# Two accumulations of the index queries use another PSUM bank

## The chip, the cores and the metric

The kernel runs on one core of a Trainium2 chip. The metric is the device time of one execution in microseconds (us), as the median of several runs. TensorE (PE below) does the matmuls, VectorE is DVE, ScalarE is ACT, GpSimd is POOL and SyncE is SP, from whose queue the transfers (DMAs) are issued. PSUM, where matmuls accumulate, has eight banks of 128 x 512 float32.

## The reference

One layer of a mixer on a sequence of 1024 rows of width 1024. After a layer norm `h`, one projection feeds four groups, A (spatial gating), B (band attention), C (sparse attention) and M (attention into 256 memory rows); each is multiplied by its SiLU gate, and an output projection and a last layer norm follow. What the change touches is the indexer of group C:

```
proj = x @ w_in + b_in          # ... iq: 8 heads of 64 columns, ik: 64 columns, iw: 8
logits = jnp.einsum('bqhd,bsd->bqhs', iqb, ikf) * (IDX_DIM ** -0.5)
score = jnp.einsum('bqhs,bqh->bqs', jax.nn.relu(logits), iwb * (IDX_HEADS ** -0.5))
_, idx = lax.top_k(score, k_sel)      # 256 keys for each query
```

The eight index heads are handled as four pairs, since two heads of 64 columns fill the 128 partitions. Below, "pair 1" to "pair 4" are the values 0 to 3 of `j` in the code.

## The kernel before, in words

Every projection is made by `project` (line 212): the weights `t` and the transposed input are each kept as a high and a low part, and for each of eight slices of the inner dimension there are three matmuls, high by high, high by low and low by high. So one piece of output columns is 24 matmuls of 512 (or 256) columns, accumulated in one PSUM bank, a tile `acc`. `wblock` (line 194) loads a block of weights; ACT makes the high part and POOL subtracts it for the low part (line 208).

The eight PSUM banks are divided by `BANKS` (line 68): two for `pp` (projections), two for `qk` and three for `pt` (scores and transposes), and one for `pv`, the value products of the attention. In the early stage there are no value products, and `pv` also serves a few other things: the SiLU projections of group A's gates (line 491), the transposed index weights (`iwt`, line 504) and the transposed spatial weights (`wst`, line 785), which ACT then copies into the tile `atab`.

The index queries: `iq_tile` (line 457) loads the weights of a pair and calls `parts_half` (line 343) for the columns 256 to 512 (the shorter piece) and then 512 to 1024 (the longer piece). `parts_half` projects, and then copies the sum out of PSUM: ACT writes the high part `iqh`, DVE the low part `iql`. Both are tiles of the tag `s4`, of which there are eight buffers (line 65), shared with `ikh`, `ikl`, `v3m`, `km`, `atab` and others; a tile gets a buffer when an earlier one has had its last reader. `index_heads` (line 464) makes the scores of a pair, row block by row block (2 and 3 together, then 4, 5, 6 and 7): 64-row matmuls `qk` of the two heads at once, ACT's relu into one of four `S` buffers, and DVE's weighted sum into `score`. `INDEX_ORDER` (line 56) is "h0 q2 h1 q3 h2 h3": the scores of pair 1, the queries of pair 3, the scores of pair 2, the queries of pair 4, then the scores of pairs 3 and 4. The queries of pairs 1 and 2 come before that. After the index part the program has `wst`, the definitions of the attention, and the gates of A (`gate_of_a`, line 487: GELU in `pp`, SiLU in `pv`, twice for each of two blocks) with the first steps of the search for the 256 largest scores.

That is the program's order. The order in which each engine takes its instructions is laid out when the kernel is built: instructions are taken by priority (the place in the program, or raised as by `BOOST_Q` for the copies of the index queries) as they become ready in a modelled time, so that later work fills the holes of earlier work. On the chip each engine then keeps to that order and waits on semaphores.

Of the kernel before, what the change touches and what calls it, by code (L numbers as in the profile page):

```python
# [24 lines left out]
P = 128  # L25
# [16 lines left out]
BOOST_Q = 2000  # L42
# [22 lines left out]
S4, EV, WB, SB, BOOST = 8, 4, 5, 4, 400  # L65
# [5 lines left out]
C_Q, C_K, C_V, C_G, I_Q, I_K, I_W, M_Q, M_G = 1792, 2048, 2304, 2560, 2816, 3328, 3392, 3400, 3656  # L71


def f32(ap):
    return ap.bitcast(F32)
# [3 lines left out]
def tile_trunk(ctx, tc, x, mem, ln_in_g, ln_in_b, w_in, b_in, a_ln_g, a_ln_b, a_ws, a_bs,  # L79
# [25 lines left out]
    def run(steps):  # L105

        while True:
            try:
                next(steps)
            except StopIteration as e:  # L110
                return e.value
# [58 lines left out]
    def s4(name, dt=F32R, shape=(P, SEQ)):  # L170
        return gp.tile(list(shape), dt, tag="s4", bufs=S4, name=name)
# [16 lines left out]
    def bank(tag, name=None):  # L188
        return ps.tile([P, 512], F32, tag=tag, bufs=BANKS[tag], name=name or tag)
# [4 lines left out]
    def wblock(w, c0, m=P):  # L194

        raw = E.tile([P, KT, P], F32, tag="raw", bufs=2, name="raw")
        loads.append(SP.dma_start(out=raw[:, :, :m], in_=w[:, c0:c0 + m].rearrange("(k p) c -> p k c", p=P)).ins)
        ts = []
        if m < P:
            narrow = [gp.tile([P, 2, KT // 2, m], F32R, tag=tag, bufs=1, name="wnar") for tag in ("planes", "score6")]  # L200
        for q in range(2):
            t = E.tile([P, 2, 4, P], F32R, tag="w", bufs=WB, name="wblk") if m == P else narrow[q]
            r = raw[:, 4 * q:4 * q + 4, :m]
            if WH[0] <= len(loads) < WH[1]:
                G.tensor_scalar(t[:, 0], r, 1.0, 0.0, ALU.mult, ALU.add)
            else:
                S.activation(t[:, 0], r, AF.Copy)
            G.tensor_sub(t[:, 1], r, f32(t[:, 0]))  # L208
            ts.append(t)
        return ts  # L210

    def project(t, a, b, m=P, hi=hh, lo=hl, tag="pp"):

        acc = bank(tag, "acc")
        for k in range(KT):
            wh, wl = t[k // 4][:, 0, k % 4, :m], t[k // 4][:, 1, k % 4, :m]
            PE.matmul(acc[:m, :b - a], wh, hi(k, a, b), start=(k == 0), stop=False)
            PE.matmul(acc[:m, :b - a], wh, lo(k, a, b), start=False, stop=False)
            PE.matmul(acc[:m, :b - a], wl, hi(k, a, b), start=False, stop=(k == KT - 1))
            yield  # L220
        return acc
# [118 lines left out]
            g = silu_of(acc, col[c0])  # L340
        SP.dma_start(out=gate_dram[kt][i], in_=g)

    def parts_half(t, c0, parts, a, b, boost=BOOST):

        hi, lo = parts
        acc = yield from project(t, a, b)
        n, bc = b - a, bias[:, col[c0]:col[c0] + 1]
        with tc.high_priority(offset=boost):
            S.activation(hi[:, a:b], acc[:, :n], AF.Identity, bias=bc)
            V.scalar_tensor_tensor(lo[:, a:b], acc[:, :n], bc, f32(hi[:, a:b]), ALU.add, ALU.subtract)  # L350
# [106 lines left out]
    def iq_tile(j):  # L457
        t = wblock(w_in, I_Q + j * P)
        q = [s4("iqh"), s4("iql")]
        for a, b in ((256, 512), (512, 1024)):  # L460
            run(parts_half(t, I_Q + j * P, q, a, b, BOOST_Q))
        return q

    def index_heads(j, q):
# [31 lines left out]

    table_parts = table_loads()
    iqs = [iq_tile(0)]
    with tc.issue_after(loads[-1]):
        for rb in range(NB):  # L500
            SP.dma_start(out=h_dram[rb], in_=xts[rb])
    tables(*table_parts)
    iqs.append(iq_tile(1))
    ptw = bank("pv", "iwt")
    for rb in range(NB):
# [12 lines left out]
    for what, j in INDEX_ORDER.split():  # L518
        j = int(j)
        if what == "q":  # L520
            iqs.append(iq_tile(j))
        if what == "h":
            index_heads(j, iqs[j])
        run(gates_of(f"{what}{j}"))
        if what == "h" and j == 3:
            for rb in RBS:
                V.memset(score[rb][0:64, (rb + 1) * P - 64:(rb + 1) * P], LOW)
# [65 lines left out]
    def parts_of(items):  # L593

        n = len(items)
        parts = []
        for t in range(n + 3):
            now, prev, prev2, prev3 = [items[t - d] if 0 <= t - d < n else None for d in range(4)]
            if now:
                parts.append(now.scores)  # L600
            if prev2:
                parts.append(prev2.values[-1])
            if prev:
                parts.append(prev.turn[0])
            if prev3 and prev3.close:
                parts.append(prev3.close)
            if prev:
                for turn, values in zip(prev.turn[1:], prev.values):
                    parts += [turn, values]
        return parts  # L610
# [156 lines left out]
    def queries_of_m(pair, q):  # L767
        wmq = wblock(w_in, M_Q + pair * P)
        q += [s4("mqh"), s4("mql")]
        for a, b in HALVES:  # L770
            yield from parts_half(wmq, M_Q + pair * P, q, a, b)
# [85 lines left out]
    class Pair:  # L857
# [13 lines left out]
        def piece(self, what, half):  # L871
            w, c = self.weight(what), self.c["qkvg".index(what)]
            if what == "q":
                if not hasattr(self, "q"):
                    self.q = [s4("qh"), s4("ql")]
                yield from parts_half(w, c, self.q, *HALVES[half])
            if what == "k":
                if not hasattr(self, "k"):
                    self.k = [s4("kh"), s4("kl")]
                yield from parts_half(w, c, self.k, *HALVES[half])  # L880
            if what == "g":
                yield from gate_half(w, c, self.kt, half)
            self.turn()
            if what == "v":
                if not hasattr(self, "v3"):
                    self.v3 = gp.tile([P, NB, 2, 3, 64], BF16, tag="v3", bufs=2, name="v3")
                acc = yield from project(w, *HALVES[half])
                with tc.high_priority(offset=BOOST):
                    vT = ev("vT")
                    S.activation(vT, acc, AF.Identity, bias=bias[:, col[c]:col[c] + 1])  # L890
                self.turned.append((vT, half))
# [410 lines left out]
    parts = parts_of(items)  # L1302
# [80 lines left out]
```

## Time and profile before

| | us |
|---|---|
| median of 3 runs | 677.58 |
| lowest, highest | 675.11, 680.07 |
| the profiled execution | 678.19 |
| its span, from the first to the last instruction | 676.4 |

| engine | busy us | share of the span | instructions |
|---|---|---|---|
| PE | 638.7 | 94% | 3698 |
| DVE | 480.1 | 71% | 1165 |
| ACT | 426.4 | 63% | 947 |
| POOL | 354.4 | 52% | 354 |

Shares are averages over stages with different limits. Matmuls follow each other in a pipeline, so that durations of single ones overlap; the spacing of their starts is what counts. A number in brackets behind an instruction in a timeline is the time for which its engine was idle before it, with what ended the idle time. The granted clock (PEclk) is 1.00 at 2.4 GHz and 0.50 at 1.2 GHz.

### The profile page before, as it was taken

To read this page: it belongs to the slowest core of one execution; us is meant where nothing else is said; L and a number is where in the kernel's file an instruction comes from. 1 tells how busy PE (TensorE), PEld (TensorE's weight loads), DVE (VectorE), ACT (ScalarE), POOL (GpSimd) and SP (SyncE) were. 2 spreads that over 40 slices of the span, in tenths; PEclk is the share of its full clock that TensorE was granted. 3 is DMA by queue.
4 is the path that set the end of the run, shared out by engine and by line. 5 is a ranking of instruction groups with operands and counts; after the bars stand their busy time and mean duration, and the time that the engine had idled before them with its cause. 6 is when DMAs were issued, how large, how long until landed. Compare 5 with 4: busy or idle time off the path is not lost.

```text
span 676.4 us, 11066 instructions
## 1 busy us (share of the span) xinstructions
PE 638.7 (94%) x3698; PEld 484.5 (72%) x3698; DVE 480.1 (71%) x1165; ACT 426.4 (63%) x947; POOL 354.4 (52%) x354
## 2 busy tenths in 40 slices
PE   4889999899999999989998999999999999999995
PEld 3867776677787677767665776667677777778785
DVE  6584256567867789899889778995567559787535
ACT  4665255547599998776879986466456575356210
POOL 3682321104535886484448535994214776557851
PEclk9999999899999999999999999999999999999999
DMA  9783521012234543554347625645101574225111
GB/s 280 236 296 112 163 57 32 0 48 63 78 110 94 110 117 97 115 123 135 71 101 139 148 74 110 120 82 150 31 16 44 180 230 145 72 88 193 66 62 63
DMA packets 121669, 75.30 MB, mean 111 GB/s; under 512 B 58976, under 2 KB 111500, under 8 KB 121612
## 3 DMA queue, kind: packets, MB, share of 16 engines
q1 hardware_dynamic: 121612, 74.59, 40.5%
q8 instruction: 29, 0.48, 0.3%
q14 instruction: 28, 0.23, 0.1%
HBM read 46.44 MB, written 17.64 MB: 95 GB/s over the span
## 4 chain that ended last, share of the span: by engine, by line
PE 50%; DVE 13%; POOL 11%; ACT 11%; issue 8%; DMA 6%; SPq 0%; POOLq 0%; DVEq 0%; ACTq 0%
PE acc L94 36%; PE qk L94 6%; ACT jka L94 4%; PE pv L94 4%; POOL wblk L208 3%; DMA pT<-sc 3%; PE pt L94 2%; DVE jk L94 2%; POOL sc L545 2%; ACT sc L94 1%; DMA raw<-in_w_in 1%; POOL sc L546 1%; DVE sc L94 1%; DMA xt<-in_x 1%; DMA hr<-h_dram 1%
## 5 line engine op out<-in xcount | busy, mean ns | idle before, releaser
L94 PE MATMUL acc<-hTh,wblk 128*128 128x512 f32 (+1 forms) x960 | 317.4, 400 | 6.4 <-DVE iql L94 2.6
L94 PEld LDWEIGHTS acc<-hTh,wblk 128*128 128x128 f32 x960 | 177.2, 189 | 52.5 <-issue 6.1
L94 PE MATMUL acc<-hTl,wblk 128*128 128x512 f32 (+1 forms) x480 | 190.4, 397 | 0.0
L208 POOL TENSOR_TENSOR wblk<-raw,wblk 128x512 fp32r<-128x512 f32 x72 | 99.7, 1388 | 123.2 <-ACT wblk L94 120.0
L94 ACT ACTIVATE jka<-score,cand 128x768 int8<-128x768 f32 (+2 forms) x93 | 96.5, 1038 | 16.2 <-DVE cand L94 15.4
L94 PEld LDWEIGHTS acc<-hTl,wblk 128*128 128x128 f32 x480 | 90.9, 189 | 20.6 <-issue 4.0
L94 PEld LDWEIGHTS <-pT 128*128 128x128 f16 x656 | 45.7, 98 | 31.7 <-issue 17.9
L94 DVE SCALAR_TENSOR_TENSOR score<-relu,iw,score 128x384 f32<-128x384 f32 (+5 forms) x42 | 43.7, 1058 | 23.9 <-ACT relu L94 22.1
L94 PE MATMUL pv<-v,pT 128*128 128x192 bf16 (+1 forms) x528 | 54.3, 234 | 4.8 <-DMA pT<-sc 4.0
L94 ACT ACTIVATE wblk<-raw 128x512 fp32r<-128x512 f32 x72 | 44.5, 627 | 22.6 <-PE acc L94 12.8
L546 POOL TENSOR_TENSOR sc<-sc 128x512 f16<-128x512 f32 (+4 forms) x48 | 56.0, 1172 | 2.3
L94 PE MATMUL acc<-woh,mh 128*128 128x512 f32 (+1 forms) x144 | 55.3, 384 | 0.0
L94 PE MATMUL acc<-wol,mh 128*128 128x512 f32 (+1 forms) x144 | 53.5, 372 | 0.0
L94 PE MATMUL acc<-woh,ml 128*128 128x512 f32 (+1 forms) x144 | 53.5, 373 | 0.0
L94 ACT ACTIVATE relu<-qk 128x384 f32<-128x384 f32 (+2 forms) x80 | 35.9, 530 | 24.1 <-PE qk L94 23.8
L545 POOL TENSOR_SCALAR sc<-sc 128x512 f16<-128x512 f32 (+4 forms) x48 | 33.4, 698 | 30.6 <-ACT sc L94 28.6
L94 ACT ACTIVATE sc<-sc,nb 128x640 f32<-128x640 f32 (+7 forms) x64 | 46.5, 729 | 1.2
L94 ACT ACTIVATE pT<-pt 128x512 f16<-128x512 f32 (+3 forms) x48 | 22.5, 485 | 31.0 <-PE pt L94 30.7
L94 ACT ACTIVATE o<-o,ri 128x64 f32<-128x64 f32 x96 | 28.1, 341 | 17.8 <-DVE o L94 17.6
L94 DVE TENSOR_SCALAR_CACHE_REDUCE jk<-planes,lo 128x384 bf16<-128x384 uint16 (+2 forms) x48 | 35.6, 742 | 1.1
L94 DVE TENSOR_SCALAR_CACHE_REDUCE jk<-planes,cand 128x384 bf16<-128x384 bf16 (+2 forms) x45 | 33.5, 744 | 1.1
L94 DVE TENSOR_REDUCE o<-pv 128x128 f32<-128x384 f32 x48 | 26.4, 549 | 9.7 <-PE pv L94 9.6
(204 smaller groups left out, 1238.4 us busy)
## 6 DMA issues: line engine op xcount, KB each, us to landing
raw<-in_w_in SPq DMA_DIRECT2D x32, 512.0 KB, 3.8
xt<-in_x SPq DMA_DIRECT2D x8, 512.0 KB, 4.7
h_dram<-xt SPq DMA_DIRECT2D x8, 512.0 KB, 5.6
gate<-t SPq DMA_DIRECT2D x16, 256.0 KB, 2.1
rawo<-in_w_out SPq DMA_DIRECT2D x8, 512.0 KB, 3.7
hr<-h_dram SPq DMA_DIRECT2D x8, 512.0 KB, 5.2
out<-hr SPq DMA_DIRECT2D x7, 512.0 KB, 2.6
gate<-gate SPq DMA_DIRECT2D x48, 64.0 KB, 2.1
```

What stands on the lines that cost most here:

```text
L94: ins = op(*a, **k)
L208: G.tensor_sub(t[:, 1], r, f32(t[:, 0]))
L545: G.tensor_scalar(high, sc[:, :n], 1.0, 0.0, ALU.mult, ALU.add)
L546: G.tensor_sub(rest, sc[:, :n], high)
```

## The change

The function `parts_half` gets an argument for the tag of the PSUM bank and hands it to `project`. `iq_tile` passes "pv" for the longer piece (`b > 512`) of the third and fourth pair (`j > 1`), and "pp", as before, for all others. Every other caller of `parts_half` keeps "pp".

```
-    def parts_half(t, c0, parts, a, b, boost=BOOST):
+    def parts_half(t, c0, parts, a, b, boost=BOOST, tag="pp"):
 
         hi, lo = parts
-        acc = yield from project(t, a, b)
+        acc = yield from project(t, a, b, tag=tag)
...
         for a, b in ((256, 512), (512, 1024)):
-            run(parts_half(t, I_Q + j * P, q, a, b, BOOST_Q))
+            run(parts_half(t, I_Q + j * P, q, a, b, BOOST_Q, "pv" if b > 512 and j > 1 else "pp"))
         return q
```

## Rows read from the trace of the kernel before

**Rows 1.** The page, parts 1 and 2: busy time, and busy tenths in 40 slices

```profile
PE 638.7 (94%) x3698; PEld 484.5 (72%) x3698; DVE 480.1 (71%) x1165; ACT 426.4 (63%) x947; POOL 354.4 (52%) x354
...
PE   4889999899999999989998999999999999999995
```

**Rows 2.** Waits of PE: who waited for whom, us in total, times, longest

```profile
PE pv L94 <- DMA pT<-sc: 5.4, 7, 1.4
PE acc L94 <- DVE iql L94: 2.6, 2, 2.1
```

**Rows 3.** Timeline of PE: start, us, instruction, count [idle before, releaser]

```profile
100.12 0.39 PE L94 MATMUL qk<-ikl,iqh 64*128 64x512 f32 x2
...
101.88 0.39 PE L94 MATMUL acc<-hTh,wblk 128*128 128x256 f32 x1 [0.58 <-DVE iql L94]
...
117.77 0.39 PE L94 MATMUL qk<-ikl,iqh 64*128 64x512 f32 x2
...
118.63 0.34 PE L94 MATMUL qk<-ikl,iqh 64*128 64x384 f32 x2
121.04 0.79 PE L94 MATMUL acc<-hTh,wblk 128*128 128x512 f32 x1 [2.07 <-DVE iql L94]
```

**Rows 4.** Windows: length, busy us (instructions) of each engine, PEclk, DMA

```profile
121.04:124.33 3.29, 3.29 (x8) 2.61 (x9) 3.29 (x4) 0.60 (x2) 0.00 (x0) 0.50 0.00 0
...
97.18:118.97 21.79, 21.14 (x140) 14.76 (x139) 13.04 (x15) 14.50 (x32) 3.85 (x3) 1.00 0.17 46
```

**Rows 5.** Windows by stage: PE, PEld, DVE, ACT, POOL, PEclk, DMA

```profile
130.00:146.00 16.00, 16.00 (x87) 11.62 (x87) 7.11 (x8) 8.21 (x18) 4.48 (x4) 1.00 0.13 34
183.00:250.00 67.00, 65.61 (x346) 51.05 (x346) 51.64 (x136) 63.45 (x144) 40.95 (x43) 1.00 0.46 113
250.00:400.00 150.00, 141.70 (x844) 104.83 (x843) 128.66 (x378) 124.09 (x288) 85.44 (x103) 1.00 0.49 112
400.00:640.00 240.00, 238.22 (x1428) 177.15 (x1427) 172.22 (x448) 135.50 (x323) 146.58 (x129) 1.00 0.38 108
```

**Rows 6.** Timeline of ACT: the copies of the queries of pairs 3 and 4

```profile
100.83 1.06 ACT L94 ACTIVATE iqh<-acc,bias 128x256 fp32r<-128x256 f32 x2
...
118.86 1.04 ACT L94 ACTIVATE iqh<-acc,bias 128x256 fp32r<-128x256 f32 x2
```

**Rows 7.** Timeline of DVE: the low parts of the same queries

```profile
101.34 1.33 DVE L94 SCALAR_TENSOR_TENSOR iql<-acc,bias,iqh 128x256 fp32r<-128x256 f32 x2
...
120.51 1.14 DVE L94 SCALAR_TENSOR_TENSOR iql<-acc,bias,iqh 128x256 fp32r<-128x256 f32 x2
```

**Rows 8.** Timeline of POOL: the last weights split before the gates of A

```profile
97.72 1.28 POOL L208 TENSOR_TENSOR wblk<-raw,wblk 128x512 fp32r<-128x512 f32 x1 [2.16 <-ACT wblk L94]
```

**Rows 9.** The chain that ended last, merged pieces: start, us, what, count

```profile
77.75 5.79 PE acc L94 x24
...
137.82 1.27 PE qk L94 x12
139.09 3.94 PE acc L94 x16
143.02 1.59 PE qk L94 x12
```

**Rows 10.** Timeline of PE: `wst`, and the first matmul of the first SiLU projection

```profile
96.76 0.49 PE L94 MATMUL wst<-ident,wsn 128*128 128x128 f32 x3
...
147.10 0.50 PE L94 MATMUL acc<-hTh,wblk 128*128 128x512 f32 x1
```

**Rows 11.** Timeline of ACT: the copy of `wst`

```profile
146.45 0.60 ACT L94 ACTIVATE atab<-wst 128x512 f32<-128x512 f32 x1 [0.43 <-PE qk L94]
```

**Rows 12.** Window of PE, matmuls that write `acc` alone

```profile
121.00:147.08 26.08, 19.63 (x72) 0.94 0.08 21
```

**Rows 13.** Timeline of DVE: pair 3's sums for row blocks 5 and 6

```profile
139.11 2.14 DVE L94 SCALAR_TENSOR_TENSOR score<-relu,iw,score 128x768 f32<-128x768 f32 x2 [2.12 <-ACT relu L94]
...
144.59 2.40 DVE L94 SCALAR_TENSOR_TENSOR score<-relu,iw,score 128x896 f32<-128x896 f32 x2 [3.33 <-ACT relu L94]
```

## The prediction

> **What bounds the kernel now.** I read the page's busy lines first, then the list of TensorE's waits, then the order of time around the index queries. The busy lines show TensorE (PE) at 638.7 us of a span of 676.4, and its row of slices at 8 or 9 tenths from the second slice on [rows 1]. So time comes back only where PE stands still or runs at its lower clock. The list of waits names a wait that belongs to the edited lines: PE, at an `acc` matmul, waits for the DVE instruction that writes `iql`, twice, 2.6 us in total, 2.1 the longest [rows 2].
>
> The PE timeline places the two: 0.58 us before the short piece of pair 4's queries at 101.88, and 2.07 us before the first GELU projection of the gates at 121.04 [rows 3]. Behind the second one the granted clock is 0.50 from 121.04 to 124.33 [rows 4]: 3.29 us at 1.2 GHz in place of 2.4, so half of it, 1.65 us, is lost. The place therefore costs 0.58 + 2.07 + 1.65 = 4.30 us. PE stands before it and after it without a hole: 16.00 of 16 us from 130 to 146, at 1.00 [rows 5].
>
> Why it waits: the two pieces of pair 3's queries fill both `pp` banks by about 97, but ACT copies them out (`iqh`, two at once) only at 100.83, and the pieces of pair 4 only at 118.86 [rows 6]. The copies go into tiles of the eight `s4` buffers. By the program's names eight are alive there (the two `ik` parts, `v3m`, `km`, the two parts of pairs 1 and 2), so pair 3's parts need the buffers of pair 1, which are read until that pair's last scores, and pair 4's those of pair 2. The times agree: by the order of the score groups pair 1's last ones start at 100.12 and pair 2's at 117.77 [rows 3]. DVE then frees the banks at 102.67 (101.34 + 1.33) and 121.65 (120.51 + 1.14), the ends of its two pairs of `iql` [rows 7]. So the banks are held by a buffer that is missing, and not by slow copies.
>
> **The change, part by part.** Matmuls, copies, tiles and DMAs are the same in number; no instruction is added, no queue (SP and POOL among them) gets another transfer or is passed by one. What moves is the bank of two 24-matmul accumulations, from `pp` to the one `pv` bank. After it the order of `pp` is pair 3 short (bank 0), pair 4 short (bank 1), first GELU (bank 0). Three consequences.
>
> *First wait.* Pair 4's short piece takes a bank that was emptied long before (pair 2's), and its weights and the next tile's are split by POOL by 99.0 (97.72 + 1.28) [rows 8]. It can run from 97 on, in the place where PE had nothing but scores and the transposes `wst`. The 0.58 goes. Its long piece must wait for `pv`, so until 102.67; ahead of that lie the last scores of pair 1, the short piece (half the columns of a long one, which takes 5.79 us for its 24 matmuls [rows 9], so 2.9) and pair 2's first scores: the scores now take from 97.18 to 101.30, where the hole begins (101.88 - 0.58) [rows 3], and 2.9 more end at 104.2. I cost that at nothing; without this cover at most 0.58 comes back.
>
> *Second wait.* The first GELU takes the bank of pair 3's short piece, free from about 102, and its weights are the tile split by 99.0 [rows 8]. It lasts 5.8 us as the long piece does and has only the copy-out of 102 ahead of it, in place of the one of 121. PE has work over the 2.07 us, and with the hole the spell of half clock should go as well. Together with the first: 4.30 back.
>
> *What is late next.* (a) `wst`, four transposes of the spatial weights in `pv`, began at 96.76 [rows 10]. It stands behind pair 4's long piece in the program, so it now runs after 121.65 and PE, which takes its order as written, can stand at it: from nothing to 121.65 - 118.97 = 2.68 us (118.63 + 0.34 being the end of the scores ahead of the hole [rows 3]). I take nothing, because the GELU's 5.8 us can lie ahead of it; the other end stays for a rival. What waits for `wst` is the copy into `atab`, and that runs at 146.45 in any case, since it needs an `s4` buffer of pair 3, free with that pair's last scores [rows 11]. (b) `pv` stays shut to the SiLU projection until then, so between 121 and 147 PE's filling is three GELU projections on `pp` and no more (72 `acc` matmuls, 3 x 24 [rows 12]); at 147.10, just behind the `atab` copy (146.45 + 0.60), the first SiLU begins [rows 10, 11]. The filling now starts earlier and ends earlier; if pair 3's scores don't move up by as much, PE runs dry ahead of them. Those scores are paced by DVE once the filling is gone: for row blocks 5 and 6 DVE takes 2.14 and 2.40 us [rows 13] where PE takes 1.27 and 1.59 [rows 9], so 0.87 + 0.81 = 1.68 us of holes if both are bare, nothing if neither is. I take 0.8, the middle, since the filling that is advanced (4.30) is about what lies between those two blocks (3.94 at 139.09 [rows 9]).
>
> Here the Trainium skill is weighed. The row: a hole of 0.58 us left the clock at 1.00 (97.18 to 118.97), the one of 2.07 did not [rows 4]. In "TensorE: Matmul & The Clock Gate", section "A second HAM failure mode: psum-queue depth-cycling", it is said that a kernel which cycles through PSUM banks leaves PE so many small holes between groups of matmuls that the clock goes up and down. By the row, (b) costs 0.8 us; by that rule its small holes would bring half-clock spells and the sum would turn positive, worked out below from rows. No row here bears the rule out for holes under 1 us.
>
> **Sum.** -4.30 + 0.8 = -3.5 us. The profiled execution took 678.19 (span 676.4), 0.61 above the median of 677.58; so 678.19 - 3.5 = 674.7, or 674.1 counted from the median. I keep 674.7. Behind 147 everything hangs on PE or on engines that follow these scores, so I let the 3.5 us stand to the end: PE is 65.61 of 67, 141.70 of 150 and 238.22 of 240 us busy in the stages up to 640 [rows 5].
>
> **Rivals.** *The wait is handed to `wst`.* The written order puts the transposes a few matmuls behind pair 2's last scores, and PE meets them before 121.65: up to 2.68 us of hole, and the half clock (1.65) behind it, 4.33 in all, against 4.30 won. For it: `wst` comes before the gates in the program, and PE's order before stood too early against the copies by those same 2.07 us. Against: before, it was laid into a gap. A change that frees PE nowhere looks the same from outside. The time is that of before, 677.6.
>
> *More than the wait goes.* From 183 to 400 PE idles 1.39 + 8.30 = 9.7 us [rows 5], in small waits such as those for `pT` [rows 2]. The written order of everything after 97 is laid anew, and if half of these waits went too: 674.7 - 4.8 = 669.9. For it: ACT is busy 63.45 of 67 us from 183 to 250, and work done earlier eases that. Against: nothing in the edit touches that stage.
>
> *Slower: pair 3's scores run bare.* The mechanism of (b), in full: the GELU projections are used up before row block 3 of pair 3 instead of beside it, the value bank is still shut, and PE goes at DVE's pace through five row blocks, 5 x 0.84 = 4.2 us of holes. With two spells of half clock as in the row, 2 x 1.65 = 3.3, this is 7.5 against 4.30: 678.19 + 3.2 = 681.4. It decides from the point where holes and spells together pass 4.30 between 119 and 147. For it: `pv` opens only with pair 3's last scores, and three projections are all there is. The rule of the Trainium skill on cycling through banks, in the section named above, would make it this case. Against: PE is full there now, and DVE (7.11 of 16 us) and ACT (8.21) have room, so that scores which come earlier on PE are taken earlier [rows 5].
>
> **How the numbers follow.** Forecast 0.45, handed to `wst` or nothing moved 0.25, more than the wait 0.12, slower 0.18. The forecast's own range, with (b) between 0 and 1.68 and a little disorder behind it, is 672 to 677. The range for 8 in 10 reaches below to the half-won waits (669.9) and above to 680.5, short of the full slower case: 669.5 to 680.5. One per cent, 6.8 us, is about what a measurement of this kernel can tell from no change (three runs lay between 675.11 and 680.07). Faster by over 1% is below 670.8: most of the third case and the edge of the first, 0.14. Slower by over 1% is above 684.4: the slower case with more holes than priced, 0.07. Within 1%: 0.79.
>
> **What would show it.** In the profile after, the wait of `acc` for `iql` is gone from the list; pair 4's short piece begins before 101; the first GELU's matmuls begin before pair 2's last scores; the granted clock is 1.00 from 97 to 147. If `wst` has the wait, a transposition with 1 to 3 us of idle time and DVE as its releaser stands near 119 to 122. If pair 3 runs bare, PE is under 15.5 of 16 us busy in the 16 us ahead of the `atab` copy. The forecast fails if that copy is not about 3 to 4 us earlier than 146.45, or if the stages behind it give the time back.

## The result and the profile after

| | before | after |
|---|---|---|
| median of 16 runs each, us | 678.61 | 675.22 |
| lowest, highest | 675.11, 684.9 | 673.33, 677.16 |
| the profiled execution, and its span | 678.19, 676.4 | 675.66, 673.9 |

The ratio is 0.9946 [0.9927, 0.9965]. The kernel is 3.4 us faster by the medians: less than the one per cent that the prediction took as its bound, but the interval leaves no room for "nothing". (Ratios below are to the kernel before, run on the same chip.)

The page of the kernel after, parts 1 and 2, answers to [rows 1]:

```profile
PE 638.5 (95%) x3698; PEld 484.8 (72%) x3698; DVE 479.7 (71%) x1165; ACT 427.0 (63%) x947; POOL 355.4 (53%) x354
...
PE   4889999999999999989899999999999999999995
PEclk9999999999999999999998999999999999999998
```

The work is the same (3698 matmuls, 638.5 us for 638.7); only the span is shorter. PE's waits after, as in [rows 2], of which the three that matter stand here:

```profile
PE pv L94 <- DMA pT<-sc: 6.5, 6, 1.4
...
PE acc L94 <- DVE iql L94: 0.3, 1, 0.3
PE acc L94 <- ACT atab L94: 0.3, 1, 0.3
```

The wait for `iql` shrank from 2.6 us to 0.3, and a wait of 0.3 for the `atab` copy is new. The timeline of PE after, to be held against [rows 3, 10], shows where both are:

```profile
96.75 0.28 PE L94 MATMUL acc<-hTh,wblk 128*128 128x256 f32 x1
...
103.98 0.50 PE L94 MATMUL acc<-hTh,wblk 128*128 128x512 f32 x1
...
110.03 0.50 PE L94 MATMUL acc<-hTh,wblk 128*128 128x512 f32 x1
...
119.53 0.50 PE L94 MATMUL acc<-hTh,wblk 128*128 128x512 f32 x1
...
127.69 0.40 PE L94 MATMUL qk<-ikl,iqh 64*128 64x512 f32 x2
...
128.94 0.50 PE L94 MATMUL acc<-hTh,wblk 128*128 128x512 f32 x1 [0.33 <-DVE iql L94]
...
135.22 0.66 PE L94 MATMUL wst<-ident,wsn 128*128 128x128 f32 x4
...
142.97 0.50 PE L94 MATMUL acc<-hTh,wblk 128*128 128x512 f32 x1 [0.29 <-ACT atab L94]
```

In order: pair 4's short piece (from 96.5; the row at 96.75 is its third matmul), the first GELU (103.98), pair 4's longer piece, now in `pv` (110.03), the second GELU, in the bank that the first has left (119.53), the last scores of pair 2 (127.69), the third GELU projection, the first of block two, which takes the bank of pair 4's short piece and waits 0.33 us for its copy-out (128.94), the transposes `wst`, with no wait (135.22), and the first SiLU, 0.29 us behind the `atab` copy (142.97). The weights tell the GELUs apart: ACT loads new ones over the two halves of block one's at 122.97 and 127.23, each just behind their use by the projection from 119.53, which is thus the last to need them. Between 96.75 and 128.61 PE has no hole. ACT's and DVE's copies of pair 4, and the `atab` copy (compare [rows 6, 7, 11]):

```profile
127.90 1.05 ACT L94 ACTIVATE iqh<-acc,bias 128x256 fp32r<-128x256 f32 x2
...
142.32 0.59 ACT L94 ACTIVATE atab<-wst 128x512 f32<-128x512 f32 x1
```

```profile
128.41 1.33 DVE L94 SCALAR_TENSOR_TENSOR iql<-acc,bias,iqh 128x256 fp32r<-128x256 f32 x2 [0.20 <-ACT iqh L94]
```

Pair 4's banks are not freed sooner: the copy runs at 127.90 in place of 118.86, and the short piece holds its bank from 96.75 on. What changed is that no one needs that bank until 128.61, because the first GELU found the other one free and the second GELU took it over from the first. Windows of the kernel after (columns as in [rows 4]):

```profile
97.00:119.00 22.00, 22.00 (x132) 16.45 (x133) 9.29 (x12) 11.28 (x24) 3.60 (x3) 1.00 0.17 45
119.00:147.00 28.00, 27.37 (x161) 19.49 (x158) 20.92 (x23) 17.98 (x40) 5.45 (x5) 1.00 0.10 28
126.30:142.30 16.00, 15.66 (x102) 10.84 (x102) 12.26 (x15) 11.11 (x25) 1.40 (x1) 1.00 0.11 32
361.00:364.30 3.30, 3.30 (x24) 2.93 (x23) 2.71 (x12) 2.79 (x8) 1.74 (x3) 0.50 0.66 125
```

The spell of half clock behind 121 [rows 4] is gone: 1.00 all through. But there is one at 361, where the profiled execution before had none.

**Where the time went, by landmarks** (start in us, the same instruction in both profiled executions):

| landmark | before | after | difference |
|---|---|---|---|
| transposed index weights, ahead of the change | 76.72 | 76.47 | -0.25 |
| `atab` copy | 146.45 | 142.32 | -4.13 |
| last scores of pair 4 | 172.4 | 168.2 | -4.2 |
| a `pv` product in the attention | 364.85 | 360.79 | -4.06 |
| the same stage, later | 417.91 | 415.42 | -2.5 |
| last matmul with `woh` | 668.5 | 665.9 | -2.6 |

In the place itself 4.13 - 0.25 = 3.88 us are won. The terms seen in the two traces make -(0.58 + 2.07 + 1.65) + 0.33 + 0.29 = -3.68, so 0.20 us are not put down to anything. The lead is carried unchanged to 361, and 1.6 us of it are lost there: half of the 3.30 us at 0.50 is 1.65. What that spell has to do with the change is the last experiment's matter.

### The profile page after: what moved, and what is told of

Its sections match the earlier page's. It is cut to its first block, busy times and chain, and to the rows that moved or that the text cites. A ratio compares the mean times of both kernels' runs of the same rounds, so it can differ in the third digit from the quotient of the medians.

```text
span 673.9 us, 11068 instructions
## 1 busy us (share of the span) xinstructions
PE 638.5 (95%) x3698; PEld 484.8 (72%) x3698; DVE 479.7 (71%) x1165; ACT 427.0 (63%) x947; POOL 355.4 (53%) x354
## 4 chain that ended last, share of the span: by engine, by line
PE 51%; DVE 12%; ACT 12%; POOL 10%; issue 7%; DMA 7%; SPq 0%; POOLq 0%; DVEq 0%; ACTq 0%
PE acc L94 36%; PE qk L94 6%; PE pv L94 5%; ACT jka L94 5%; DMA pT<-sc 3%; POOL wblk L208 3%; PE pt L94 3%; DVE jk L94 2%; POOL sc L546 2%; ACT sc L94 1%; DMA raw<-in_w_in 1%; DMA xt<-in_x 1%; DMA hr<-h_dram 1%; POOL rs L134 1%; ACT relu L94 1%
```

## The experiments

The theory: PE stood still because a `pp` bank was held past the end of pair 2's scores by a copy-out that had no `s4` buffer to write to; the half clock came from the hole; and it is pair 4's longer piece that cures it, by leaving the bank to the GELU. Rivals: the order of all later work, laid anew, or fewer changes between projections and scores, made the gain; or the half clock belongs to the place and not to the hole.

**One piece at a time.** In `only_pair3` the third pair's longer piece alone goes to `pv`, in `only_pair4` the fourth's alone.

```
only_pair3:  ..., "pv" if b > 512 and j == 2 else "pp"))
only_pair4:  ..., "pv" if b > 512 and j == 3 else "pp"))
```

> Only pair 3's longer piece goes to the value bank; pair 4's stays in a pp bank. Theory (what costs is a pp bank held over the end of pair 2's scores): the first GELU then takes the bank of pair 4's short piece and still waits for its copy-out, so the hole of about 2.07 us and the half-clock spell stay; only the 0.58 us hole near 102 goes. The copy into atab is at 145.5 to 146.5, the time within 0.8 us of the kernel before. Rival (the new order of scores and fillers, and the transposes wst taken out of the gap at 97, bring the gain): wst moves here too, so about half or more of the 3.4 us should come, 2 us or more.

> Only pair 4's longer piece goes to the value bank. Theory: the first GELU takes the bank of pair 3's longer piece, free at about 102.7, so the hole before it is gone, and with pair 4's longer piece in the value bank PE has work near 97 too; the waits of acc for iql are under 0.7 us in sum (2.6 before), the granted clock is 1.00 from 97 to 147, the copy into atab is 3.3 to 4.2 us earlier than 146.45, and the time is that of the kernel after, 3 to 4 us under before. Rival (both moves are needed, since the value bank only helps when pair 3's piece has opened a pp bank): half of the gain or less, under 1.8 us.

`only_pair3` measured 676.83 us, ratio 0.9986 [0.9968, 1.0004]: no gain that the interval bears out (by the ratio 0.95 us, where at most 0.8 was expected). PE's timeline, and a window behind it:

```profile
120.09 0.50 PE L94 MATMUL acc<-hTh,wblk 128*128 128x512 f32 x1 [1.92 <-DVE iql L94]
```

```profile
121.05:124.35 3.30, 3.30 (x10) 2.56 (x9) 3.09 (x4) 0.00 (x0) 0.00 (x0) 0.51 0.00 0
```

The hole of 2 us stays, with the half clock behind it, and the `atab` copy comes only 0.9 us sooner (145.54). `only_pair4` measured 675.08, ratio 0.9949 [0.9931, 0.9967], all that the whole change gives. Its PE has no wait for `iql` at all; the `atab` copy is at 142.86 and only the SiLU's hole is left:

```profile
143.50 0.50 PE L94 MATMUL acc<-hTh,wblk 128*128 128x512 f32 x1 [0.30 <-ACT atab L94]
```

So the half of the edit that concerns the third pair is not needed.

These two also answer the rival of fewer changes between projections and scores. From the landmark at 76 to the last scores of pair 4, the timelines of PE have 23 separate stretches of scores before and 22 after; `only_pair3`, without the gain, has 22 too, and `only_pair4`, with all of it, has 25.

**The other cure.** If the bank is held for want of a buffer, then a buffer must do as much as a bank. Both of these kernels keep all banks as before and put the query parts of one pair into a tag whose two buffers lie idle at that time.

```
-        q = [s4("iqh"), s4("iql")]
+        q = [gp.tile([P, SEQ], F32R, tag="v3", bufs=2, name=n) if j == 2 else s4(n) for n in ("iqh", "iql")]
```

(`pair3_other_buffers`; `pair4_other_buffers` has `j == 3`.)

> The banks are those of the kernel before; pair 3's two query parts go into two buffers that lie idle at this time (those of the value tiles of B) in place of s4 buffers, so that ACT and DVE can copy pair 3 out as soon as it is summed, and pair 4 into the buffers of pair 1. Theory (the banks are held because a buffer is missing): the copies of pair 3 follow their pieces at about 90 and 97, those of pair 4 come near 105 and not 118.9, no wait of acc for iql over 0.5 us, granted clock 1.00 from 97 to 147; pair 4's last scores 3 to 4.5 us earlier than 172.4. The order of everything behind is laid anew, so the time may differ from the kernel after by some us; 672 to 678. Rival (copies are slow or queue behind relus, the buffers do not matter): copies at 100.8 and 118.9 as before, hole of about 2 us stays.

> The banks of the kernel before; only pair 4's two query parts go into the two idle buffers, pair 3's stay in s4 buffers and are copied out with the end of pair 1's scores. Theory: the bank that costs is the one held over the end of pair 2's scores; pair 4's copies now follow its pieces (before 115, not at 118.9), so the hole of 2.07 us and its half-clock spell are gone while the one of 0.58 near 102 stays, with no bank moved. Gain 3 to 4 us against the kernel before, like the kernel after. Rival (the gain needs the value bank as a third bank): hole and spell stay, gain under 1 us.

`pair3_other_buffers`: 675.59 us, ratio 0.9951 [0.9933, 0.9969]. ACT's copies there, pair 3's and then pair 4's:

```profile
89.11 0.48 ACT L94 ACTIVATE iqh<-acc,bias 128x256 fp32r<-128x256 f32 x1
...
96.54 0.69 ACT L94 ACTIVATE iqh<-acc,bias 128x512 fp32r<-128x512 f32 x1 [2.00 <-PE acc L94]
...
103.61 0.48 ACT L94 ACTIVATE iqh<-acc,bias 128x256 fp32r<-128x256 f32 x1
...
110.79 0.69 ACT L94 ACTIVATE iqh<-acc,bias 128x512 fp32r<-128x512 f32 x1 [1.45 <-PE acc L94]
```

Before, two copies stood together because both had waited for the same buffer (x2 in [rows 6]). Now each follows its own piece, and where it waits it is for PE. PE has no hole in 76 us:

```profile
97.00:119.00 22.00, 22.00 (x129) 15.59 (x128) 10.93 (x14) 11.80 (x26) 4.13 (x3) 1.00 0.15 42
119.00:147.00 28.00, 28.00 (x142) 19.16 (x141) 14.21 (x15) 15.08 (x31) 7.12 (x7) 1.00 0.12 37
147.00:173.00 26.00, 26.00 (x137) 18.43 (x136) 16.80 (x25) 16.14 (x33) 12.39 (x9) 1.00 0.22 65
```

One part of the expectation missed: the last scores of pair 4 come at 182.8, ten us later than before and not earlier, as the new order puts projections ahead of them. The total is won all the same, so those scores do not set the end.

`pair4_other_buffers`: 674.11 us, ratio 0.9943 [0.9924, 0.9962]. Here the small hole, which belongs to pair 3's copy, stays, and the large one is gone (timeline and windows of PE):

```profile
101.37 0.39 PE L94 MATMUL acc<-hTh,wblk 128*128 128x256 f32 x1 [0.58 <-DVE iql L94]
```

```profile
119.00:147.00 28.00, 28.00 (x148) 20.82 (x147) 14.88 (x15) 15.65 (x32) 8.07 (x7) 1.00 0.17 48
420.00:480.00 60.00, 53.98 (x297) 39.01 (x298) 54.31 (x113) 31.69 (x70) 31.02 (x25) 0.97 0.40 96
```

A buffer thus removes the hole that the bank removes: the cause is the buffer that was missing. That the totals agree as well is in part luck. By the sixth of ACT's copies `kh`, `pair4_other_buffers` is 10.5 us ahead of the kernel before (401.2 for 411.7) and `pair3_other_buffers` 8.1 (403.6), far more than the holes were worth; their waits for `pT` are down to 0.9 and 1.2 us from 5.4 [rows 2], in another order of work. The second row shows where it goes again. From 420 to 480 PE is busy 53.98 of 60 us (59.24 before), with three waits of 1.65 to 1.93 us that the kernel before does not have there, and a spell of half clock behind the last of them; `pair3_other_buffers` has the same three (1.65, 1.93 and 1.76) and a spell at 466.8. The tag also serves value tiles of the attention (line 886), and the order of the later work fell out otherwise; which of the two makes these waits was not tried apart.

**Both cures together.** `after_and_pair4_buffers` is the changed kernel with the `j == 3` buffers.

> The kernel after, with pair 4's two query parts in the two idle buffers besides. Nothing of PE's queue then waits for a bank between 97 and 147 (0.33 us for iql and 0.29 us for atab in the kernel after). Theory (PE was left 0.62 us of holes there and is else full): at most 1 us better than the kernel after, so 673.5 to 676, ratio to the kernel before 0.993 to 0.996. Rival (the order matters beyond the holes: groups of scores that stay together cost PE less than groups that alternate with projections, and this order has the fewest alternations of all so far): 2 us or more better than the kernel after, under 673.

674.46 us, ratio 0.9949 [0.9933, 0.9966]. Its windows of PE:

```profile
97.00:119.00 22.00, 22.00 (x129) 16.55 (x128) 10.68 (x15) 12.03 (x26) 2.68 (x3) 1.00 0.17 47
119.00:147.00 28.00, 28.00 (x156) 20.59 (x155) 15.02 (x16) 16.11 (x34) 8.06 (x7) 1.00 0.11 30
420.00:480.00 60.00, 54.91 (x295) 39.78 (x294) 53.65 (x109) 33.19 (x74) 30.05 (x24) 0.94 0.42 99
```

The last 0.6 us of holes in the place go, but the stage from 420 on loses more. This is no better than either cure, and neither it nor any other kernel of the study beats the changed one beyond the intervals.

**Filling the hole, and what the clock does.** Three kernels keep the banks and buffers of before and put matmuls whose results nobody reads ahead of the first GELU, which still has to wait for the copy-out. If the half clock comes from the hole, filling it must keep the clock at 1.00 and give about 1.65 us; if it belongs to the place, it stays.

```
+            if j == 1:                       # behind pair 2's scores
+                hold = bank("pt", "hold")    # "qk" in hole_filled_scores_bank
+                for i in range(8):           # 4 in hole_half_filled
+                    ... PE.matmul(hold, hh(i, 0, P), hh(i, 0, 512), start=(i == 0), stop=(i == 7))
```

> The kernel before with eight matmuls of 512 columns into a scores bank, read by nobody, placed on PE right behind pair 2's last scores, where the hole of 2.07 us is: 8 x 0.233 = 1.9 us of work that buys nothing. Theory: the half clock from 121.0 to 124.3 follows from the hole, so with the hole filled the clock stays at 1.00 while the first GELU still starts at about 121; 1.65 us of the gain comes back and pair 4's last scores are 1 to 1.7 us earlier than 172.4. Rival (the half clock there has other causes, such as the thin 64-row matmuls before it): the clock falls as before and the landmark stays within 0.4 us, or is later.

> As hole_filled, eight matmuls read by nobody behind pair 2's last scores, but in a bank of the tag qk; here the groups of scores stay in pairs behind it, as in the kernel before, where hole_filled had split them. Theory: filled hole, granted clock 1.00 from 119 to 147, the first GELU begins near 121 as before and the 1.65 us of the spell come back: the copy into atab 1.0 to 1.8 us earlier than 146.45, the time 0.5 to 2 us under the kernel before. What hole_filled lost was the splitting of pairs. Rival (the half clock cost nothing that PE would not have waited for anyway): the copy into atab within 0.4 us of 146.45 and the time no better.

> As hole_filled with four matmuls in place of eight, so that a hole of about 1.0 us is left behind them; the order behind it is nearly that of the kernel before. If the half clock follows from the length of the hole alone, as the 0.58 us hole left it at 1.00 and 1.92 and 2.07 did not, then 1.0 us lies between and this run says on which side: with the clock at 1.00 the copy into atab is 1 to 1.8 us earlier than 146.45, with a spell of half clock it stays within 0.5 us.

`hole_filled`: 680.32 us, ratio 1.0026 [1.0011, 1.004], slower. The clock did what the theory says (timeline of the fillers, and a window):

```profile
117.90 2.11 PE L94 MATMUL hold<-hTh 128*128 128x512 f32 x8
```

```profile
119.00:147.00 28.00, 27.89 (x139) 18.50 (x139) 15.30 (x17) 13.12 (x28) 4.94 (x4) 1.00 0.07 20
```

Yet the `atab` copy came at 146.88, not earlier. The order laid behind the fillers was another: pairs of score groups that had run together were split, with projections between them. Two timeline rows of `hole_filled` give the price:

```profile
135.11 0.44 PE L94 MATMUL qk<-ikh,iqh 64*128 64x384 f32 x2
...
135.83 0.50 PE L94 MATMUL acc<-hTh,wblk 128*128 128x512 f32 x1
```

Six score matmuls alone take 0.72 us here, where twelve in a row took 1.27 [rows 9], and the change from `acc` to `qk` adds about 0.1 (0.33 against a spacing of 0.23): some 0.27 us more for each pair that is split. Up to pair 4's last scores there are 29 stretches of scores for 23 before, so 1.6 us. From the landmark at 76 to those scores it takes 0.6 us longer than before (96.2 for 95.6), where the clock alone would have made it 1.65 shorter; so the order accounts for 1.6 of 2.2 us, and the rest is open. Nor is that what made the total slower, by the two traces: at ACT's fourth copy `kh` this kernel is 1.0 us ahead (358.8 for 359.8), and at the sixth, behind a spell of half clock from 364.0, it is 1.2 us late (412.9 for 411.7). So this run doesn't isolate the clock.

`hole_filled_scores_bank`, whose fillers stand in a score bank so that the pairs stay together: 678.44 us, ratio 1.0005 [0.9992, 1.0017]. The clock is 1.00 again, with 0.76 us of hole left, and the `atab` copy is at 145.62, which is 0.5 us sooner counted from the landmark at 76 (76.38 there). That is a third of what was expected, and the total shows nothing: a miss. About 0.65 us of it can be placed: pair 3's first group of scores, which before ran ahead of the hole (from 118.18), now runs behind the start of the GELU (at 124.87, the next group at 125.52). As for the total, this kernel too is ahead (357.5 for 359.8 at the fourth copy `kh`), has a spell of half clock from 362.6, and is level at the sixth (411.7); the rest isn't placed.

`hole_half_filled`, with half of the fillers, is the cleaner one (24 stretches of scores), at 675.06 us, ratio 0.9952 [0.9934, 0.9971]. Timeline and windows of PE:

```profile
118.26 1.20 PE L94 MATMUL hold<-hTh 128*128 128x512 f32 x4
...
121.21 0.50 PE L94 MATMUL acc<-hTh,wblk 128*128 128x512 f32 x1 [1.03 <-DVE iql L94]
```

```profile
119.00:122.00 3.00, 1.97 (x11) 1.17 (x11) 2.90 (x5) 2.81 (x7) 0.00 (x0) 1.00 0.00 0
122.00:126.00 4.00, 4.00 (x23) 3.04 (x23) 3.27 (x4) 0.10 (x1) 0.00 (x0) 1.00 0.00 0
```

The GELU begins at 121.21, not earlier than before (121.04); a hole of 1.03 us is left; the clock is 1.00; and the `atab` copy comes at 145.10, 1.35 us sooner, or 1.5 from the landmark at 76 (76.89). So with a shorter hole in the same place the half clock is gone, and that is worth about 1.5 us by itself (priced 1.65, measured in one trace). The rest of this kernel's 3.3 us came behind the place: between 333 and 348 two waits for `pT` of 0.47 and 0.48 us are gone, which the fillers can have touched by way of the order alone; some 0.9 us are not put down to anything.

**The same kernels a second time,** one execution each, to see which spells of half clock belong to a program.

```
before_again: the kernel before        after_again: the changed kernel
```

> The kernel before once more, for its trace. Theory: hole of 2.0 to 2.1 us before the first GELU and a spell of half clock of about 3.3 us behind it, as in the first trace, so the two belong to the program and not to one execution. Rival: the spell depends on the execution, then the clock may be 1.00 here and the copy into atab is near 144.8 in place of 146.45.

> The kernel after once more, for its trace. In the first trace it was 4.1 us ahead up to 359 and 2.5 ahead from 365 on, with a spell of half clock from 361.0 to 364.3 behind holes that the kernel before has too. If that spell belongs to one execution, the clock is 1.00 there this time and the lead stays near 4 us; if it belongs to the program, it is there again. The copy into atab is at 142 to 142.6 and the clock 1.00 from 97 to 147 in either case.

`before_again` took 678.05 (span 676.3). Its PE timeline and a window:

```profile
120.42 0.50 PE L94 MATMUL acc<-hTh,wblk 128*128 128x512 f32 x1 [2.07 <-DVE iql L94]
```

```profile
121.35:124.60 3.25, 3.25 (x10) 2.56 (x9) 3.12 (x4) 0.00 (x0) 0.00 (x0) 0.54 0.00 0
```

Hole and spell stand again where they stood. `after_again` took 673.38 (span 671.6), with its `atab` copy at 142.41, and the window at 361:

```profile
361.00:364.30 3.30, 3.30 (x30) 2.50 (x31) 2.92 (x16) 2.84 (x8) 1.90 (x2) 1.00 0.66 131
```

The same two holes stand ahead of it as in the first execution (0.90 and 0.66 for 0.92 and 0.67), and the clock is 1.00. So the changed kernel does not have the spell at 361 in every execution. But the first one was no single case either. Windows of `only_pair4`, `hole_filled` and `hole_filled_scores_bank`:

```profile
361.20:364.50 3.30, 3.04 (x22) 2.66 (x24) 2.61 (x13) 2.85 (x6) 2.24 (x3) 0.50 0.70 148
...
364.00:367.30 3.30, 3.30 (x25) 2.84 (x23) 2.75 (x13) 2.95 (x8) 1.90 (x3) 0.50 0.66 126
...
362.60:365.90 3.30, 3.30 (x24) 2.92 (x26) 2.62 (x13) 2.87 (x8) 1.91 (x2) 0.50 0.66 130
```

Of the six traces without a spell at 121 (the two other-buffer kernels and their combination with the change aside) four have one here, and the three with a spell at 121 have none. Whether a spell that is removed at 121 makes one near 361 more likely these nine traces can't say; if it does, the change hands part of the 1.65 us on. The granted clock of whole executions gives an idea of it: 0.9942 on average in 16 of the changed kernel, 0.9923 in 43 of the kernel before. By an estimate from these, 0.0019 of 675 us, some 1.3 us less are lost to half clock over all stages.

Single spans say little about the size of the gain. The second execution of the changed kernel is 4.7 us under `before_again` (676.3 - 671.6), the first 2.5 us under its own (676.4 - 673.9), but one more execution of the kernel before, run beside these last two, took 675.29 (span 673.5), only 1.9 us more than `after_again`.

## Why the prediction was right

**The wait and its cause.** As worked out: the banks were held by a buffer that was missing, not by slow copies. The two other-buffer kernels show it: they touch no bank, the copies of the pair so treated follow its pieces, and the hole of 2.07 us with its half clock is gone.

**First wait, 0.58.** Gone, for the reason given: pair 4's short piece begins at 96.5. Its longer piece did not follow at 104 but at 110.03, behind the start of the first GELU; with `pv` free from about 104.4 that cost nothing.

**Second wait, 2.07, and the half clock, 1.65.** Gone, and `hole_half_filled` measures the second at about 1.5. The first GELU begins before pair 2's last scores, as was said. What was not foreseen is that those scores come ten us later (127.69 for 117.77), with two GELUs and both pieces of pair 4 ahead of them. So pair 4's buffers, and its short piece's bank, come free later than before, and the wait for `iql` was not gone from the list but left at 0.33 us, ahead of the third GELU projection.

**(a) `wst`, taken as nothing.** Right: the transposes run at 135.22 without a wait, and the rival of the wait handed on falls.

**(b) Pair 3's scores bare, taken as 0.8.** The size was near (0.62), but by luck, for the make-up was another. The scores did run bare: of pair 3's, with pair 4's first group, 48 matmuls stand in a row from 136.73 to the SiLU at 142.97. But no hole in the profile comes from DVE's pace: PE is busy 15.66 of the 16 us ahead of the `atab` copy, with the 0.33 inside them. What is there are the 0.33 for the bank of pair 4's short piece and the 0.29 for the `pv` bank at the SiLU. The slower rival, made of the same mechanism, falls with it: DVE is busy 20.92 us from 119 to 147 (14.97 before), so scores that are taken earlier are indeed summed earlier. One reading behind the 0.8 was off: the 1.59 us of PE [rows 9] are two groups of 512 columns, the second half of row block 6 and the first of 7, and not the 896 columns of block 6, so that the second excess (0.81) was priced too low.

**The rule on small holes.** The Trainium skill, "TensorE: Matmul & The Clock Gate", section "A second HAM failure mode: psum-queue depth-cycling", reports of a kernel that cycles through PSUM banks that its clock went up and down, as PE idled briefly and often between groups of matmuls. Holes of 0.29 to 1.03 us at bank changes stand in both executions of the changed kernel and in `hole_half_filled`, two in each, and their clock from 97 to 147 was 1.00; so these traces do not bear it out at this size and number, and the prediction was right to leave it a rival.

**The sum.** -3.5 us forecast, -3.4 by the medians and 675.22 for 674.7. That the two agree to 0.1 us is luck: the place gave 3.9, somewhat more, and later stages vary by one to two us between orders and executions, which the prediction let pass as "a little disorder". The spell near 361 is part of that, and the prediction had no term for half clock elsewhere. The last rival, that the later waits would go as well, has nothing for it: waits for `pT` are 6.5 us for 5.4 in the profiled executions and 5.7 for 6.4 in the second ones.

## What to carry to other kernels

Where PE waits for a copy out of PSUM, ask what the copy waits for: when two copies run back to back long after their matmuls ended, it is their destination, and then one more buffer, or another bank for the work that is queued behind, removes the wait. Where the trace shows half clock behind a hole, count it with the hole, here 1.65 us on 2.07; but look whether other traces show it there too, since holes of the same size elsewhere left the clock alone. Judge such an edit by a landmark just behind its place, since here the later stages moved by as much as the gain.

## What was not expected of the hardware

The granted clock did not follow the size of a hole. Holes of 1.92 and 2.07 us ahead of the first GELU were followed by some 3.3 us at 0.50 to 0.54 in all three traces that have them, and holes of 0.58, 0.76 and 1.03 left it at 1.00. But elsewhere holes as long mostly left it alone. The kernel before has one of 2.04 us at 33.67, and `pair4_other_buffers` one of 1.93 at 457.95 (PE, then the windows behind):

```profile
33.67 0.46 PE L94 MATMUL acc<-hTh,wnar 128*72 128x512 f32 x1 [2.04 <-ACT wnar L94]
...
33.67:36.97 3.30, 3.30 (x15) 2.00 (x16) 3.30 (x7) 1.43 (x3) 3.28 (x4) 1.00 0.16 30
```

```profile
457.95 0.33 PE L94 MATMUL pt<-ident,o 128*128 128x128 f32 x1 [1.93 <-ACT o L94]
...
458.00:461.30 3.30, 3.04 (x15) 2.25 (x15) 3.23 (x3) 1.56 (x3) 1.66 (x1) 1.00 0.60 164
```

The hole near 33 is 1.56 to 2.21 us long in the twelve traces, and a spell follows in two (`hole_filled_scores_bank`, `hole_half_filled`); one of about 1.7 us near 303 is in nine, and a spell follows in one (`hole_half_filled`). In turn, two holes of 0.92 and 0.67 us near 360, with two us of work between them, brought a spell in one execution of the changed kernel and none in the other (0.90 and 0.66); the kernel before has them too (0.86 and 0.66, at 362.89 and 364.85) and ran on at 1.00 (250 to 400 [rows 5]). What decides between them stays open. So the hole ahead of the GELU was needed for the half clock at 121, but a hole of that size is not enough by itself.

Changes between 64-row score matmuls and 128-row projections have a price on PE itself, about 0.27 us for each pair of score groups that is split. In `hole_filled`, six more stretches of scores took back 1.6 us, about what the removed half clock was worth.
